# Preparation of a chunked RWKV-7 branch: wide matmuls between the chunk products, inverse and values on four array tiles, and a written order behind the inverse

## The chip, the cores and the metric

The kernel runs on one core of one Trainium2 chip. The metric is the device time of one execution in microseconds; a figure for a kernel is the median of its runs. Numbers of a trace are those of one profiled execution. The engines are named as in the profile: PE is TensorE's matmuls, PEld its weight loads, DVE VectorE, ACT ScalarE, POOL GpSimd, SP SyncE, which issues nearly all DMAs.

## The reference

One layer of a decoder on 1024 tokens of 1024 channels: three branches on one normalised input (causal pooling, RWKV-7, cross attention into 256 memory tokens), gates, an output projection, and a convolutional FFN. The change lies in the RWKV-7 branch, whose recurrence runs over tokens, with a 64x64 state in each of 16 heads:

```python
def step(state, inp):
    rt, wt, kt, vt, an, bn = inp
    sa = jnp.einsum('bhvk,bhk->bhv', state, an)
    state = state * wt[:, :, None, :] + sa[..., None] * bn[:, :, None, :] + vt[..., None] * kt[:, :, None, :]
    yt = jnp.einsum('bhvk,bhk->bhv', state, rt)
    return state, yt
...
kk = kk * lax.rsqrt(jnp.sum(kk * kk, axis=-1, keepdims=True) + L2_EPS)
w_log = -jax.nn.softplus(-(w0 + jnp.tanh(dw) @ w_up_decay).astype(f32)) - 0.5
a = jax.nn.sigmoid((a0 + da @ w_up_a).astype(f32))
```

## The kernel before, in words

Tokens are cut into 16 chunks of 64, so the recurrence becomes matrix products within a chunk, a triangular inverse per chunk and head, and a walk over the 16 chunks. Full precision comes from splitting each fp32 operand into a high and a low part: one product of a 128x128 weight tile with 512 tokens is a **wide triple**, three matmuls (`mm3`, lines 180 to 182). An fp32 operand that isn't split makes the chip run two matmuls for one in the code, so the trace counts twice what the code writes.

In time, the program is: the start; four **groups** of preparation (`rwkv_group`, two pairs of heads each, `i` = 0 and 1); the walk (`chain`); attention, pooling, gates and FFN. A group does, in the code's order:

- **lengths** (`square_sums`, 464 to 473): ACT squares the keys twice, once rounded into `sp[:, 0]` and once in full into a half of `tHV`; DVE subtracts the two into `sp[:, 1]`; PE sums over channels into `phd` (two matmuls a half, bank pool `pss`); ACT turns that into a reciprocal root, by Ln and Exp, back into `tHV` (`rstd`).
- **up-projections** (496 to 504): eight pairs of matmuls `psu`, each followed by a Sigmoid on ACT; then the table of activation functions goes back to Ln and Exp. The two banks of pool `g0` are shared with `in_block`.
- **r and scaling** (525 to 554): for each `i` a projection `in_block` of 48 wide matmuls, and some ten operations of DVE and ACT that make `AR`, `BK` and `kv`.
- **values** (`pv`, 570 to 581): 64x64 products with `cent` that centre the values into `HV`, then its store to HBM (`spill`).
- **chunk products** (`ps`, 588 to 610): for each `i` four bursts of four chunks. A burst writes two PSUM banks (`ps1`, `ps2`); ACT copies one half of each bank (605, 608) and DVE masks the rest out of them (606, 607, 609, 610). Four banks are rotated, so a third burst needs the banks of the first. Behind them stand a bonus (`pbo`), scaling and transposes (`pt`) and stores.
- **solve** (647 to 664): 31 steps on DVE invert the diagonal 32x32 blocks and end in eight copies into `NTu`, the last of which is `place`.
- **inverse** (`pz`, `pw`, 665 to 682): 32x32 products complete the 64x64 inverses, in two halves of 16 chunks: `pz`, a copy by ACT and one by DVE into `Z`, `pw`, copies by ACT into `NT`. `NT` is then stored (line 693, `d_nt`).

Two sources of wide triples that nothing near them needs fill PE under the solve: keys and values of the next group (`group_kv`, 64 triples a group), and the projections whose results are spilled for later (`fill_to`, 32 jobs of 16 triples, lines 861 to 888). `fill_to(48 * (g + 1))` asks for 48 more in each group. A scheduler then places all of this on the engines' queues by its own estimate of times; `later(a, b)` only says that `a` stands behind `b`.

SBUF buffers go by tags: two tiles with one tag share one slot, and a new tile's first write waits until all readers of the tile before it are done, its stores included. `tHV` and, after it, `HV` hold the slot "HV"; `NT` holds the slot "NT". In the walk, `pair` takes "HV" and `state` takes "NT".

Of the kernel before, what the change touches and what calls it, by code (L numbers as in the profile page):

```python
# [17 lines left out]
P = 128  # L18
# [3 lines left out]
C = 64  # L22
# [8 lines left out]
LAST = HK - 4  # L31

# [12 lines left out]
def trunk_kernel(ctx: ExitStack, tc: tile.TileContext, xT, memT, pvec, w_in, w_kv, w_upd, w_upg,  # L45
# [416 lines left out]
    def square_sums(src, scale, sq, sp):  # L462
# [6 lines left out]
        for n, (t0, _) in enumerate(HALVES):  # L469
            ps = pss.tile([P, 512], F32, name="phd", tag="s")  # L470
            PE.matmul(ps, bonesr, sp[:, 0, t0:t0 + 512], start=True, stop=False)
            PE.matmul(ps, bonesr, sp[:, 1, t0:t0 + 512], start=False, stop=True)
            yield slice(t0, t0 + 512), ps

    def rwkv_group(g, kv):
# [10 lines left out]

        def lengths():
            for i in range(2):
                for s, ps in square_sums(kv[i][:, 0], col("k_k", 2 * g + i), tHV[:, i, 1], sp[:, i]):
                    rstd(tHV[:, i, 1, s], ps, 1)  # L490

        if g:
            lengths()
            table(SIGMOID)
        for i in range(2):
            p = 2 * g + i
            uh, ul = load_up2(w_upd[p])
            for t0, _ in HALVES:
                s = slice(t0, t0 + 512)
                for e, l, dst, b in ((0, ld, tBN[i][:, 0, s], "w0"), (1, la, tHV[:, i, 0, s], "a0")):  # L500
                    ps = psg.tile([P, 512], F32, name="psu", tag="g0")
                    PE.matmul(ps, uh[:, e], l[:, s], start=True, stop=False)
                    PE.matmul(ps, ul[:, e], l[:, s], start=False, stop=True)
                    act(dst, ps, AF.Sigmoid, bias=col(b, p))
        table(LN_EXP)
        if g == 0:
            lengths()
        AR = rw.tile([P, 2, 3, T], F32, name="AR", tag="AR")
        vs = []
# [7 lines left out]

        for i in range(2):
            p = 2 * g + i
            t0_, t1_ = kv[i][:, 0], kv[i][:, 1]  # L520
# [13 lines left out]
            in_block(8 + p, shifted(p, r_))  # L534

# [18 lines left out]
            vs.append(t1_)  # L554

        def bonus(i):

            t0_ = kv[i][:, 0]
            for t0, _ in HALVES:
                s = slice(t0, t0 + 512)  # L560
                ps = pss.tile([P, 512], F32, name="pbo", tag="s")
                PE.matmul(ps, bones, t0_[:, s], start=True, stop=True)
# [7 lines left out]
        NT = rw.tile([P, 2, NCH, C], F32, name="NT", tag="NT")  # L570
        HV = rw.tile([P, 2, NCH, C], F32, name="HV", tag="HV")
        for i in range(2):
            for c0 in (0, 8):
                ps = pss.tile([P, 8, C], F32, name="pv", tag="s")
                for c in range(8):
                    tsl = slice((c0 + c) * C, (c0 + c + 1) * C)
                    PE.matmul(ps[64:128, c], vs[i][0:64, tsl], cent[0:64], start=True, stop=True)
                    PE.matmul(ps[0:64, c], vs[i][64:128, tsl], cent[64:128], start=True, stop=True)
                A.copy(HV[64:128, i, c0:c0 + 8], ps[64:128])
                A.copy(HV[0:64, i, c0:c0 + 8], ps[0:64])  # L580
            spill(d_hv, (g, i), HV[:, i])

# [6 lines left out]
        for i in range(2):  # L589
            us = slice(NCH * i, NCH * i + NCH)  # L590
            for c0 in range(0, NCH, 4):
# [5 lines left out]
                m = None  # L597
                for c in range(4):
                    t = slice((c0 + c) * C, (c0 + c + 1) * C)
                    for e, rows in ((1, up), (0, lo)):  # L600
                        m, was = PE.matmul(ps[e][:, c], BK[i][rows, c0 + c], AR[rows, i, e:e + 2, t],
                                           start=True, stop=True), m
                        if was is not None:
                            later(m, was.ins)
# [22 lines left out]
            for c0 in range(0, NCH, 4):  # L627
                ps = pss.tile([P, 4, P], F32, name="pt", tag="s")
                for c in range(4):
                    PE.transpose(ps[:, c], BK[i][:, c0 + c], ident)  # L630
# [27 lines left out]
        fill_to(48 * (g + 1))  # L658
        if g == 3:
            w_queue[0] = A  # L660
            fill_to(256, solve)
        for us in (slice(0, NCH), slice(NCH, 2 * NCH)):
            for q, (qs, bs) in enumerate(quads):
                place = V.tensor_copy(NTu[qs, us, bs], X[qs, us]).ins
        Z = tmp
        ends = [(slice(e, e + 32), slice(e + 32, e + 64)) for e in (0, 64)]
        for u0 in (0, 16):
            us = slice(u0, u0 + 16)
            ps = pss.tile([P, 16, 32], F32, name="pz", tag="s")
            for u in range(16):  # L670
                for q0, q1 in ends:
                    m = PE.matmul(ps[q1, u], NTu[q0, u0 + u, 32:64], S11[q0, u0 + u], start=True, stop=True)
                    if u0 == u == 0:
                        later(m, place)
            A.copy(Z[32:64, us], ps[32:64])
# [1190 lines left out]
```

## Time and profile before

| what | before |
|---|---|
| median of 3 runs | 1940.28 us (1934.13 to 1942.58) |
| profiled execution, its own time | 1933.07 us |
| its span | 1931.4 us |
| PE, DVE, ACT, POOL busy | 97%, 71%, 54%, 41% |
| the four groups, first to last | 94 us to 665 us of the span |
| the walk | 665 us to 858 us |

The profiled execution took 1.7 us more than its span, and lies 7.2 us under the median. In the trace "start us, us" are an instruction's start and duration; a bracket is the time that its engine sat idle before it and what ended that. A matmul's duration contains the array's latency, so the rate is read from the distance between starts.

### The profile page before, as it was taken

To read this page: it belongs to the slowest core of one execution; us is meant where nothing else is said; L and a number is where in the kernel's file an instruction comes from. 1 tells how busy PE (TensorE), PEld (TensorE's weight loads), DVE (VectorE), ACT (ScalarE), POOL (GpSimd) and SP (SyncE) were. 2 spreads that over 40 slices of the span, in tenths; PEclk is the share of its full clock that TensorE was granted. 3 is DMA by queue.
4 is the path that set the end of the run, shared out by engine and by line. 5 is a ranking of instruction groups with operands and counts; after the bars stand their busy time and mean duration, and the time that the engine had idled before them with its cause. 6 is when DMAs were issued, how large, how long until landed. Compare 5 with 4: busy or idle time off the path is not lost.

```text
span 1931.4 us, 33821 instructions
## 1 busy us (share of the span) xinstructions
PE 1869.7 (97%) x12204; PEld 1515.9 (78%) x12204; DVE 1366.2 (71%) x2054; ACT 1048.7 (54%) x2190; POOL 785.7 (41%) x867
## 2 busy tenths in 40 slices
PE   8999999998999999999999999999999999999997
PEld 6767877876777888788788888888788888888886
DVE  8677677677677446657964534679798888877798
ACT  6685385385484355555664345555454454544544
POOL 4422221222221211121323455566599888821441
PEclk9999999999999999999999999999999999999999
DMA  5326236326239669975246444653322222289775
GB/s 165 130 73 184 93 88 179 100 77 186 94 95 303 207 195 317 329 220 183 96 139 207 130 131 141 194 164 123 105 85 90 86 80 85 88 263 211 170 189 144
DMA packets 269641, 296.28 MB, mean 153 GB/s; under 512 B 18336, under 2 KB 219168, under 8 KB 266400
## 3 DMA queue, kind: packets, MB, share of 16 engines
q1 hardware_dynamic: 248480, 271.56, 44.5%
q0 software_dynamic: 11856, 14.16, 4.5%
q10 hardware_dynamic: 9136, 8.39, 1.5%
q8 instruction: 96, 1.57, 0.3%
q14 instruction: 73, 0.60, 0.1%
HBM read 207.00 MB, written 87.03 MB: 152 GB/s over the span
## 4 chain that ended last, share of the span: by engine, by line
PE 65%; DVE 5%; DMA 3%; ACT 1%; issue 1%; POOL 0%; SPq 0%; DVEq 0%; ACTq 0%; POOLq 0%
PE psg L180 11%; PE psg L182 11%; PE psg L181 11%; PE psf L182 6%; PE psf L180 6%; PE psf L181 6%; PE psd L181 3%; PE psd L182 3%; PE psd L180 3%; PE py L780 1%; DMA R<-d_f 1%; PE pr L780 1%; PE ph L780 1%; DMA hv<-d_hv 1%; DMA gt<-d_bv 1%
## 5 line engine op out<-in xcount | busy, mean ns | idle before, releaser
L139 POOL TENSOR_TENSOR wlo<-wraw,whi 128x256 fp32r<-128x256 f32 x464 | 403.9, 883 | 827.1 <-ACT whi L132 772.8
L180 PE MATMUL psg<-hh,whi 128*128 128x512 f32 x928 | 373.9, 403 | 12.7 <-ACT whi L132 8.5
L182 PE MATMUL psg<-hh,wlo 128*128 128x512 f32 x928 | 368.7, 398 | 1.6 <-POOL wlo L139 1.4
L181 PE MATMUL psg<-hl,whi 128*128 128x512 f32 x928 | 369.0, 398 | 0.3 <-DVE hl L266 0.2
L132 ACT CAST whi<-wraw 128x256 fp32r<-128x256 f32 x472 | 181.5, 403 | 246.1 <-PE psg L181 96.1
L180 PEld LDWEIGHTS psg<-hh,whi 128*128 128x128 f32 x928 | 175.7, 189 | 55.8 <-ACT whi L132 14.4
L182 PEld LDWEIGHTS psg<-hh,wlo 128*128 128x128 f32 x928 | 176.0, 190 | 42.6 <-POOL wlo L139 4.9
L181 PEld LDWEIGHTS psg<-hl,whi 128*128 128x128 f32 x928 | 176.0, 190 | 36.7 <-issue 1.4
L1192 POOL TENSOR_TENSOR wt<-a,wt 128x256 fp32r<-128x256 f32 x136 | 155.5, 1167 | 35.3 <-ACT wt L1191 35.3
L181 PE MATMUL psd<-f,u 128*128 128x512 f32 x292 | 114.0, 390 | 0.5 <-DVE f L1608 0.4
L180 PE MATMUL psd<-f,u 128*128 128x512 f32 x292 | 113.2, 391 | 1.2 <-ACT f L1604 1.2
L182 PE MATMUL psd<-f,u 128*128 128x512 f32 x292 | 113.7, 389 | 0.0
L182 PE MATMUL psf<-h2h,wt 128*128 128x512 f32 x272 | 105.9, 389 | 0.1
L180 PE MATMUL psf<-h2h,wt 128*128 128x512 f32 x272 | 105.9, 389 | 0.0
L181 PE MATMUL psf<-h2l,wt 128*128 128x512 f32 x272 | 105.8, 389 | 0.0
L1206 DVE SCALAR_TENSOR_TENSOR d<-z,pv,d 128x1023 f32<-128x1023 f32 x68 | 101.1, 1491 | 2.1
L1192 POOL TENSOR_TENSOR wt<-s,wt 128x256 fp32r<-128x256 f32 x68 | 81.2, 1213 | 2.8 <-ACT wt L1191 1.9
L181 PE MATMUL psf<-t,wt 128*128 128x512 f32 x204 | 79.4, 389 | 0.0
L180 PE MATMUL psf<-t,wt 128*128 128x512 f32 x204 | 79.4, 389 | 0.0
L182 PE MATMUL psf<-t,wt 128*128 128x512 f32 x204 | 79.4, 389 | 0.0
L1204 ACT ACTIVATE d<-z,pv 128x1024 f32<-128x1024 f32 x34 | 42.4, 1247 | 65.7 <-DVE z L1286 49.9
L1191 ACT CAST wt<-a 128x256 fp32r<-128x256 f32 x136 | 50.7, 404 | 40.8 <-POOL wt L1192 25.9
(436 smaller groups left out, 4499.2 us busy)
## 6 DMA issues: line engine op xcount, KB each, us to landing
wraw<-in_w_in SPq DMA_DIRECT2D x176, 128.0 KB, 2.4
a<-in_w_fup SPq DMA_DIRECT2D x128, 128.0 KB, 2.4
d_ar<-AR SPq DMA_DIRECT2D x24, 512.0 KB, 4.2
d_zg<-st SPq DMA_DIRECT2D x48, 256.0 KB, 3.5
ring<-d_ar SPq DMA_DIRECT2D x8, 1536.0 KB, 11.9
wraw<-in_w_fup SPq DMA_DIRECT2D x80, 128.0 KB, 2.5
fraw<-d_f SPq DMA_DIRECT2D x33, 256.0 KB, 4.1
d_rb<-RB SPq DMA_DIRECT2D x16, 512.0 KB, 5.7
```

The lines of the kernel that those rows point to most:

```text
L132: i = A.copy(hi, src)
L139: (V if lo_on_dve[0] else G).tensor_tensor(lo, src, hi.bitcast(F32), op=ALU.subtract)
L180: first = PE.matmul(ps, wh, xh, start=start, stop=False)
L181: PE.matmul(ps, wh, xl, start=False, stop=False)
L182: last_mm[0] = PE.matmul(ps, wl, xh, start=False, stop=stop).ins
L780: m = PE.matmul(out_, l, r, **kw)
L1191: A.copy(w[0][:, us], src[u])
L1192: low = eng.tensor_tensor(w[1][:, us], src[u], w[0][:, us].bitcast(F32), op=ALU.subtract)
L1204: A.activation(d, z, AF.Identity, scale=col("cw2", j), bias=col("cb", j))
L1206: V.scalar_tensor_tensor(d[:, n:], z[:, :T - n], col(cw, j), d[:, n:], op0=ALU.mult, op1=ALU.add)
```

## The change

1. **Values** move ahead: they are made after the `in_block` of `i` = 0 (new `values()`), all four quadrants of the array in turn, a half of the chunks in each of two banks, each product ordered behind the one before.
2. **Slots are swapped**: `HV` now takes the slot "NT", and `NT` takes the slot "HV", which it shares with `tHV`.
3. **Inverse**: the two halves of `pz`, and of `pw`, are interleaved, so that four 32x32 tiles take turns in one bank; the second stage is ordered behind the copies of the first.
4. **Chunk products**: a burst stands as one row, with one wide triple after the first and two after the second and third (`covered`); one triple stands ahead of each later bonus product and of four transposes in group 3.
5. **Behind the inverse**: four triples behind `place`, two within the lengths of `i` = 1, ten among the up-projections. For this 16 triples of groups 0 to 2 are left to the next group (`LEFT`); the sum stays 48 a group. In `square_sums` the order of the two products is turned.

The core of the diff:

```diff
+GROUP, LEFT = 48, 16
+TAKEN = 4 * GROUP + 64
...
         for n, (t0, _) in enumerate(HALVES):
             ps = pss.tile([P, 512], F32, name="phd", tag="s")
-            PE.matmul(ps, bonesr, sp[:, 0, t0:t0 + 512], start=True, stop=False)
-            PE.matmul(ps, bonesr, sp[:, 1, t0:t0 + 512], start=False, stop=True)
+            if n == 0 and ahead is not None:
+                wide = ahead()
+            m = PE.matmul(ps, bonesr, sp[:, 1, t0:t0 + 512], start=True, stop=False)
+            if n == 0 and ahead is not None:
+                later(m, wide)
+            last_sum_[0] = PE.matmul(ps, bonesr, sp[:, 0, t0:t0 + 512], start=False, stop=True).ins
...
+        cover, burst = [GROUP * g - LEFT if g else 0], [None]
+
+        def covered(n, behind=None):
+            cover[0] += n
+            fence[0] = behind
+            wide = fill_to(cover[0])
+            fence[0] = None
+            return wide
+
         if g:
+            covered(4, placed[0])
             lengths()
             table(SIGMOID)
+        raised = [0, last_sum_[0]]
...
-                    PE.matmul(ps, uh[:, e], l[:, s], start=True, stop=False)
-                    PE.matmul(ps, ul[:, e], l[:, s], start=False, stop=True)
+                    m = PE.matmul(ps, uh[:, e], l[:, s], start=True, stop=False)
+                    if g and 2 <= raised[0] < 7:
+                        later(m, covered(1 if raised[0] > 2 else 6, raised[1]))
+                    m = PE.matmul(ps, ul[:, e], l[:, s], start=False, stop=True)
+                    raised[:] = raised[0] + 1, m.ins if raised[0] > 1 else raised[1]
...
+        def values():
+
+            lo, up = slice(0, 64), slice(64, 128)
+            HV = rw.tile([P, 2, NCH, C], F32, name="HV", tag="NT")
+            after = last_mm[0]
+            for i in range(2):
+                ps = [pool.tile([P, 8, C], F32, name="pv", tag=tag)
+                      for pool, tag in (((psk, "k"), (psc, "c")) if i else ((pss, "s"), (pss, "s")))]
+                for c in range(8):
+                    for n in (1, 0):
+                        t = slice((8 * n + c) * C, (8 * n + c + 1) * C)
+                        for rows, at_ in ((lo, lo if n else up), (up, up if n else lo)):
+                            m = PE.matmul(ps[n][at_, c], vs[i][rows, t], cent[rows], start=True, stop=True)
+                            later(m, after)
+                            after = m.ins
+                for n in range(2):
+                    A.copy(HV[up, i, 8 * n:8 * n + 8], ps[n][lo if n else up])
+                    A.copy(HV[lo, i, 8 * n:8 * n + 8], ps[n][up if n else lo])
+                spill(d_hv, (g, i), HV[:, i])
+            return HV
...
             in_block(8 + p, shifted(p, r_))
+            if i == 0:
+                HV = values()
...
-        NT = rw.tile([P, 2, NCH, C], F32, name="NT", tag="NT")
-        HV = rw.tile([P, 2, NCH, C], F32, name="HV", tag="HV")
+        NT = rw.tile([P, 2, NCH, C], F32, name="NT", tag="HV")
...
-                m = None
+                after = covered(min(2, c0 // 4), burst[0]) if c0 else None
...
+                        if after is not None:
+                            later(m, after)
+                        after = m.ins
+                burst[0] = after
...
-        fill_to(48 * (g + 1))
+        fill_to(GROUP * (g + 1) - (LEFT if g < 3 else 0))
...
+        us = slice(0, 16), slice(16, 32)
+        ps = pss.tile([P, 16, 32], F32, name="pz", tag="s")
+        for u in range(16):
+            for h in range(2):
+                for ends_ in ends:
+                    m = PE.matmul(ps[ends_[1 - h], u], NTu[ends_[0], 16 * h + u, 32:64],
+                                  S11[ends_[0], 16 * h + u], start=True, stop=True)
...
+        for h in range(2):
+            moved = [A.copy(Z[32:64, us[h]], ps[ends[0][1 - h]]),
+                     V.tensor_copy(Z[96:128, us[h]], ps[ends[1][1 - h]])]
+        ps = pss.tile([P, 16, 32], F32, name="pw", tag="s")
+        for u in range(16):
+            for h in range(2):
+                for ends_ in ends:
+                    m = PE.matmul(ps[ends_[h], u], Z[ends_[1], 16 * h + u],
+                                  NTu[ends_[1], 16 * h + u, 32:64], start=True, stop=True)
+                    for i in moved:
+                        later(m, i.ins)
+        for h in range(2):
+            for ends_ in ends:
+                A.copy(NTu[ends_[0], us[h], 32:64], ps[ends_[h]])
...
-    chain(lambda v: 279 + 121 * (v - 1) // 46 if v else 262)
+    chain(lambda v: TAKEN + 23 + (377 - TAKEN) * (v - 1) // 46 if v else TAKEN + 6)
```

The last line yields the same numbers as before. Where the scheduler now puts the instructions is seen at three places. The rows are those of an engine's queue in the built program; numbers behind a name count buffers, and a name of a semaphore behind "waits" is an engine's or, with DMAHW, a DMA queue's.

First, PE at the first chunk products of group 1, before (a burst is eight rows of two banks' names; "..." leaves out its repeats):

```order
L181 MATMUL psg<-hl,whi 128x512
L601 MATMUL ps_2705<-AR,BK_2337 128x128
L601 MATMUL ps_2704<-AR,BK_2337 128x128
...
L601 MATMUL ps_2721<-AR,BK_2337 128x128
L601 MATMUL ps_2720<-AR,BK_2337 128x128
...
L182 MATMUL psg<-hh,wlo 128x512
L601 MATMUL ps_2737<-AR,BK_2337 128x128
```

And after the change, from the end of the first burst:

```order
L641 MATMUL ps_2702<-AR,BK_2255 128x128
L182 MATMUL psg<-hh,whi 128x512
L183 MATMUL psg<-hl,whi 128x512
L184 MATMUL psg<-hh,wlo 128x512
L641 MATMUL ps_2719<-AR,BK_2255 128x128
```

Before, two bursts stand together, then one wide matmul, then the next two; now 3, 8 and 6 wide matmuls stand between the bursts of `i` = 0, and 3, 6 and 6 for `i` = 1.

Second, ACT behind the inverse of group 0, before: the squares for group 1 stand far ahead, and the copies of the inverse are followed by Ln and Exp on `phd`.

```order
L467 ACTIVATE sp_2333<-kv1_1712,pv_88 128x512 [waits DVE_49,Activation_49]
L467 ACTIVATE tHV_2336<-kv1_1712,pv_88 128x512
...
L675 COPY tb1_1875<-pz_2261 32x512 [waits PE_49]
L682 COPY NT_1223<-pw_2296 32x16x32 [waits PE_49]
L682 COPY NT_1223<-pw_2296 32x16x32
L214 ACTIVATE tHV_2336<-phd_2345,eps_114 128x512 [waits PE_49]
```

After the change (the `sp` squares still stand ahead, the `tHV` ones don't):

```order
L723 COPY tb1_1937<-pz_2111 32x512 [waits DVE_49]
L735 COPY NT_1330<-pw_2180 32x16x32 [waits PE_49]
L735 COPY NT_1330<-pw_2180 32x16x32 x3
L471 ACTIVATE tHV_2254<-kv0_1611,pv_88 128x512 [waits DMAHW1_49,DMAHW0_49,Activation_49]
L471 ACTIVATE tHV_2254<-kv1_1774,pv_88 128x512 x2
L216 ACTIVATE tHV_2254<-phd_2300,eps_114 128x512 [waits DVE_49,PE_49]
```

The four squares into `tHV` have moved behind the copies into `NT`, and the first of them now waits for two DMA queues.

Third, PE at the same place, before:

```order
L680 MATMUL pw_2296<-NT_1223,tb1_1875 32x32 x30
L471 MATMUL phd_2345<-sp_2333,bonesr_95 128x512 [waits PE_49]
L472 MATMUL phd_2345<-sp_2333,bonesr_95 128x512
L182 MATMUL psg_3364<-hh_146,wlo_3348 128x512
L180 MATMUL psg_3364<-hh_146,whi_3353 128x512
```

After the change:

```order
L718 MATMUL pz_2111<-tb1_1937,NT_1330 32x32 x63
L182 MATMUL psg_2281<-hh_146,whi_2258 128x512 [waits Activation_49]
...
L729 MATMUL pw_2180<-NT_1330,tb1_1937 32x32 x60
L525 MATMUL psu_2340<-ld_219,uhi_2334 128x512
L528 MATMUL psu_2344<-la_220,ulo2_221 128x512
L477 MATMUL phd_2300<-sp_2251,bonesr_95 128x512 [waits DVE_49,PE_49]
L480 MATMUL phd_2300<-sp_2251,bonesr_95 128x512
```

The first sum of the lengths has stayed right behind the inverse, with two pairs of up-projections between; its wait now names DVE, whose subtraction needs the squares. Nine wide matmuls stand between `pz` and `pw`.

More of the change, by code (lines that the diff above doesn't have):

```diff
@@ L485, in rwkv_group, with between @@
         BKs = [rw.tile([P, NCH, P], F32, name=f"BK{i}", tag=tagB[i]) for i in range(2)]
+        def between():
+            return covered(2, last_sum_[0])
         def lengths():
             for i in range(2):
-                for s, ps in square_sums(kv[i][:, 0], col("k_k", 2 * g + i), tHV[:, i, 1], sp[:, i]):
+                for s, ps in square_sums(kv[i][:, 0], col("k_k", 2 * g + i), tHV[:, i, 1], sp[:, i],
+                                         between if g and i else None):
                     rstd(tHV[:, i, 1, s], ps, 1)
+        cover, burst = [GROUP * g - LEFT if g else 0], [None]
[5 more added lines that the diff above has]
+            return wide
         if g:
+            covered(4, placed[0])
             lengths()
             table(SIGMOID)
+        raised = [0, last_sum_[0]]
         for i in range(2):
@@ L507, in rwkv_group @@
             lengths()
+            covered(1)
         AR = rw.tile([P, 2, 3, T], F32, name="AR", tag="AR")
-        vs = []
+        vs = [kv[i][:, 1] for i in range(2)]
         turn = [0]
@@ L561, in bonus @@
                 ps = pss.tile([P, 512], F32, name="pbo", tag="s")
-                PE.matmul(ps, bones, t0_[:, s], start=True, stop=True)
+                m = PE.matmul(ps, bones, t0_[:, s], start=True, stop=True)
+                if g == 3 and (i or t0):
+                    later(m, covered(1, burst[0]))
+                burst[0] = m.ins
                 V.tensor_tensor(t0_[:, s], vs[i][:, s], ps, op=ALU.mult)
@@ L600, in rwkv_group @@
                     for e, rows in ((1, up), (0, lo)):
[L601 to L604, printed above, removed]
+                        m = PE.matmul(ps[e][:, c], BK[i][rows, c0 + c], AR[rows, i, e:e + 2, t],
+                                      start=True, stop=True)
+                        if after is not None:
+                            later(m, after)
+                        after = m.ins
+                burst[0] = after
                 A.copy(RB[i][:, 0, cs], ps[0][:, :, 1])
@@ L629, in rwkv_group @@
                 for c in range(4):
-                    PE.transpose(ps[:, c], BK[i][:, c0 + c], ident)
+                    m = PE.transpose(ps[:, c], BK[i][:, c0 + c], ident)
+                    if c == i == 0 and g == 3:
+                        later(m, covered(1, burst[0]))
+                burst[0] = m.ins
                 A.copy(BKN[i][:, c0:c0 + 4], ps)
@@ L875, in fill_steps @@
                     later(m, behind)
+                if fence[0] is not None:
+                    later(m, fence[0])
                 filled.append(last_mm[0])
```

38 lines of the change are left out of this document (8 added, 30 removed).

## The prediction

> **What bounds the kernel now.** I read the page's busy times first, then its chain of waits, then PE's busy time by stretches of group 1 and group 2, then the timeline of PE inside each stretch, with DVE's and ACT's beside it. The first two, from the page:
>
> ```profile
> span 1931.4 us, 33821 instructions
> PE 1869.7 (97%) x12204; PEld 1515.9 (78%) x12204; DVE 1366.2 (71%) x2054; ACT 1048.7 (54%) x2190; POOL 785.7 (41%) x867
> PE 65%; DVE 5%; DMA 3%; ACT 1%; issue 1%; POOL 0%; SPq 0%; DVEq 0%; ACTq 0%; POOLq 0%
> ```
>
> PE is the bound: 65% of the chain, and the next engine has 5%. But "busy" counts a matmul's latency, so I look at what a stretch achieves. The windows are: the inverse of group 1, from there to the first chunk product of group 2, its chunk products up to the solve, and the chunk products and solve of group 1 (PE busy and count, PEld, DVE, ACT, POOL, granted clock, DMA share, GB/s):
>
> ```profile
> 372.81:381.72 8.91, 8.91 (x273) 6.95 (x272) 1.39 (x2) 3.12 (x6) 0.72 (x1) 1.00 0.41 127
> 381.72:425.25 43.53, 42.64 (x293) 33.35 (x289) 30.69 (x32) 38.24 (x56) 11.74 (x11) 1.00 0.24 69
> 425.25:455.72 30.47, 24.95 (x195) 18.27 (x195) 17.38 (x36) 22.57 (x58) 2.92 (x4) 1.00 0.64 192
> 283.73:314.45 30.72, 25.74 (x196) 18.98 (x195) 18.20 (x38) 22.57 (x58) 2.93 (x4) 0.97 0.64 191
> 314.45:372.81 58.36, 57.53 (x257) 46.86 (x256) 51.22 (x101) 22.23 (x46) 19.61 (x26) 0.99 0.41 124
> ```
>
> Only the chunk products leave PE idle, about 5.5 us of 30.5. Under the solve PE is full, so every wide matmul moved out of there to a gap shortens the solve's stretch, until DVE's chain is late. The unit price of that is the pitch of wide matmuls; the prices of the small products stand in the same timeline:
>
> ```profile
> 420.65 0.39 PE L182 MATMUL psg<-hh,wlo 128*128 128x512 f32 x1
> ...
> 422.24 0.39 PE L180 MATMUL psg<-hh,whi 128*128 128x512 f32 x1
> 422.56 0.27 PE L577 MATMUL pv<-cent,kv 64*64 64x64 f32 x1
> ...
> 424.66 0.22 PE L577 MATMUL pv<-cent,kv 64*64 64x64 f32 x1
> 424.67 0.22 PE L578 MATMUL pv<-cent,kv 64*64 64x64 f32 x1
> 424.82 0.50 PE L181 MATMUL psg<-hl,whi 128*128 128x512 f32 x1
> 425.25 2.09 PE L601 MATMUL ps<-AR,BK 64*128 64x128 f32 x32
> ...
> 678.54 0.69 PE L780 MATMUL pu<-Rs,pair 64*64 64x64 f32 x32
> 679.16 0.50 PE L180 MATMUL psg<-hh,whi 128*128 128x512 f32 x1
> ```
>
> From 420.65 to 422.24 seven wide matmuls start, 0.227 us apart. Into a block of small ones and out of it the step is longer: 422.24 to 422.56 is 0.32, 424.82 to 425.25 is 0.43. I take 0.3 us for a block's two borders together.
>
> **Values: -9.7.** They are 128 matmuls in the trace, 64 pairs of two row tiles, a pair each 0.058 us (32 pairs and the way out fill the 2.26 us from 422.56 to 424.82; less 0.3 that is 1.9, or 0.06 a pair), so 3.8 us, in three blocks of about 0.3: 4.7 a group. After the change one block has quartets. The walk's `pu` works on four quadrants: 32 matmuls and the switch out in 0.62 us (678.54 to 679.16), which is 8 quartets of about 0.058. So 32 quartets are 1.9 us, with a border 2.2. The gain is 2.5 in groups 1 to 3. In group 0 the values lay in two blocks, and I take 2.2 there: 9.7.
>
> **Inverse: -10.4.** The 8.91 us of the window hold 273 matmuls: 4 `psu` (0.91), 11 wide ones (2.50), the rest (258, of which 256 are the inverse) takes 5.5. Its rate:
>
> ```profile
> 372.81 1.20 PE L672 MATMUL pz<-tb,NT 32*32 32x32 f32 x64
> 373.94 0.50 PE L502 MATMUL psu<-ld,uhi 128*128 128x512 f32 x1
> ```
>
> 64 matmuls in 1.13 us is 0.032 a pair, with about 0.1 of border: 128 pairs are 4.1, and five blocks about 1.4. As quartets, 64 of 0.032 are 2.05, with three blocks (the wide triples split `pw`) 0.85: 2.9. The gain is 2.6, four times: 10.4. The copies between `pz` and `pw` now all stand ahead of `pw`: two of DVE at half of the window's 1.39, two of ACT at half of the 1.17 quoted below, 2.6 if none overlap. Nine wide matmuls behind `pz` (2.0) and the three that follow `pw`'s first rows (0.7) cover them, so I cost them at nothing; bare they would cost 2.6 a group.
>
> **Chunk products: -14.4.** These rows are the bursts of group 2, first of `i` = 0, then of `i` = 1, and what DVE does at their start:
>
> ```profile
> 427.26 0.51 PE L182 MATMUL psg<-hh,wlo 128*128 128x512 f32 x1
> 429.17 1.16 PE L601 MATMUL ps<-AR,BK 64*128 64x128 f32 x16 [1.40 <-DVE AR L610]
> 430.92 1.16 PE L601 MATMUL ps<-AR,BK 64*128 64x128 f32 x16 [0.60 <-DVE AR L610]
> 432.85 1.10 PE L562 MATMUL pbo<-kv,bonesr 128*128 128x512 f32 x2 [0.33 <-DVE AR L610]
> 448.13 2.06 PE L601 MATMUL ps<-AR,BK 64*128 64x128 f32 x32
> 456.81 0.41 PE L630 MATMUL pt<-ident,BK 128*128 128x128 f32 x2 [0.59 <-DVE AR L610]
> ```
>
> ```profile
> 421.31 1.64 DVE L553 TENSOR_TENSOR AR<-AR,tBN 128x1024 f32<-128x1024 f32 x1
> 427.29 0.43 DVE L609 TENSOR_TENSOR NT<-ps,mstrict 64x256 f32<-64x256 f32 x1 [4.33 <-ACT RB L608]
> ```
>
> The four bursts of `i` = 0 take 7.60 us (425.25 to 432.85). Two wide matmuls lie in it, 0.45; 7.15 is bursts and waits. After the change 17 wide ones lie in it. Sixteen matmuls start over about 0.9 us, so with a border for each burst the four are 4.7; the third still waits some 1.2 for the masks of the first, since four masks of 0.43 are 1.74 and the fill before it is 11 x 0.227 = 2.5 and starts before the masks do. That makes 5.94 beside the 17: a gain of 1.2. For `i` = 1 it is 8.68 us (448.13 to 456.81) with 4 wide, 7.77 otherwise; after, 15 wide and 5.35 otherwise (the masks are clear of AR's work there): 2.4. Together 3.6 a group, 14.4. The wide matmuls themselves are not a gain: they are missing later.
>
> **The new wait: +20.1.** `tHV` now takes the slot in which `NT` was, so the first square into `tHV` waits until both stores of the previous group's `NT` have landed. Behind it on ACT stand all of Ln, Exp and the sigmoids; on PE the sum `phd` waits for it at the head of the queue. The rows, around the end of group 1's inverse (381.72):
>
> ```profile
> 381.72 0.50 PE L471 MATMUL phd<-sp,bonesr 128*128 128x512 f32 x1
> 394.95 0.40 PE L180 MATMUL psg<-hh,whi 128*128 128x512 f32 x1
> ```
>
> ```profile
> 381.82 1.17 ACT L682 COPY NT<-pw 32x512 f32<-32x512 f32 x2 [2.69 <-PE pw L680]
> 383.01 0.69 ACT L214 ACTIVATE tHV<-phd,eps 128x512 f32<-128x512 f32 x1
> ...
> 387.81 1.28 ACT L208 ACT_TABLE_LOAD   x1
> ```
>
> ```profile
> d_nt<-NT SPq DMA_DIRECT2D x8, 512.0 KB, 3.2
> L467 ACT ACTIVATE tHV<-kv,pv 128x512 f32<-128x512 f32 x16 | 11.4, 719 | 2.2 <-ACT whi L132 2.0
> L468 DVE TENSOR_TENSOR sp<-tHV,sp x16: 628/790/1223, 81.9 to 485.2; 128x512 fp32r<-128x512 f32 x16
> ```
>
> Before, `phd` starts as soon as the inverse ends, T; ACT's eight Ln and Exp fill T+1.3 to T+6.1, and the r products begin at T+13.2 (394.95). After: four copies by ACT, half of 1.17 each, end at T+2.4; the store lands 3.2 later, T+5.7; a square (0.72) makes it T+6.4, with issue up to T+6.9; DVE's subtraction (0.63 to 0.9) T+7.6; `phd` starts at T+7.7. Until then PE has the four matmuls of two `psu`, about 1.0, and idles some 6.6 us. On ACT, Ln and Exp then begin at T+8.2 and take 4.8, the table 1.28, the first sigmoid 0.69: T+15.0. The `psu` behind it rotate two banks, so the next six come in steps of a triple and a pair (5 x 0.227 = 1.14, I take 1.2): T+22.2, and only then does the first r product get its bank. From there PE has 96 wide matmuls of r (21.8), the values (2.2) and borders (0.6): the first chunk product starts at T+46.8. Before it starts at T+43.5, with 8 more wide matmuls ahead of it (1.8), the values' 2.5 (counted above) and without the four `psu` of 0.91 that lay in the inverse's window: like for like 40.1. The wait costs 6.7 at each of three boundaries (ahead of groups 1, 2 and 3): 20.1. Its ends: 4.5 a boundary, if two thirds of the idle remain, and 9.0, the whole shift of the r products.
>
> Beside that, the Trainium skill: "TensorE: Matmul & The Clock Gate", in its part on the clock gate, says that an idle window of about 3.4 us halves PE's clock until as long a busy one is through; by it each of the three idles would cost up to about 1.7 us more (an estimate from that page), and the sum would be -8, and the time 1932. No idle of before is that long in the groups; its chunk products, idle for 5 of 30 us in pieces up to 1.4, show 0.97 once and 1.00 once at 30.72 and 30.47 us, so at most 0.25 there.
>
> **Small costs: +1.3.** In group 0 the first bursts stand ahead of 36 wide matmuls of `i` = 1's projection, and BK's copies behind eight of the values': 0 to 3.3, I take 1.0. The walk's start: 0.3 (0 to 1).
>
> **The solve: 0.** DVE's last copies end before `pz` by:
>
> ```profile
> 217.53 4.78 DVE L664 COPY NT<-tb 32x512 f32<-32x512 f32 x8
> 364.88 3.48 DVE L664 COPY NT<-tb 32x512 f32<-32x512 f32 x8
> 231.30 1.20 PE L672 MATMUL pz<-tb,NT 32*32 32x32 f32 x64
> ```
>
> In group 0 that is 231.30 - 222.31 = 9.0 us, in group 1 372.81 - 368.36 = 4.45. After the change PE reaches `pz` 263 - 216 = 47 wide matmuls (10.7 us) sooner in group 0, and 239 - 221 = 18 (4.1) in group 1 (numbers of wide matmuls between the last burst and `pz`, counted in PE's order); but DVE no longer does the next group's four subtractions (4 x 0.8 = 3.2) in that stretch, and the bursts' masks end earlier. I leave it at nothing; the bound is 1.7 in group 0 and 1 in each of two groups, about 3.
>
> Sum: -9.7 - 10.4 - 14.4 + 20.1 + 1.3 = **-13.1 us**. The profiled execution took 1933.07, 1.7 more than its span, and lies 7.2 under the median of 1940.28; the change gives 1920 against the one, and **1927 against the median**, which I forecast.
>
> **Rivals.** A difference of 0.5%, 9.7 us, is about what a measurement of this kernel can tell from no change.
>
> *The tiles of the inverse don't overlap, since they write one bank.* `pz` and `pw` have all four tiles in one bank, and half the quartet shares the rows of the other half. Then only the borders are saved: 1.4 - 0.85 = 0.55 a group, 2.2 in place of 10.4, the sum -4.9, 1935: same. For it: nothing in this trace has four tiles in one bank at 32x32. Against it: two row tiles into one bank start 0.01 us apart at 424.66 and last 0.22 each. By the Trainium skill, "TensorEngine Tiling (Array Packing)", "Gotcha 1: PSUM Pressure", different row tiles cannot access one bank at the same time; that pair of rows speaks against the rule for two. Chance 0.13.
>
> *Evacuation bounds the chunk products.* If the bursts wait for masks and copies at their own pace, the wide matmuls between them only take the place of idle time that the next wait gives back: no 14.4, the sum +1.3, 1942: same. For it: each wait's releaser is DVE or ACT. Against: ACT is busy 22.57 of 30.47 us and DVE 17.38, so neither is full. Chance 0.13.
>
> *The wait is covered*, because the up-projections and the fill run on while ACT waits: without the 20.1, the sum is -33, 1907. Against it: PE's queue is in order, and `phd` stands at its head. Chance 0.07.
>
> *The store lands late, and the change is slower.* At T+2.4 the two stores meet the other traffic of that place, weights and up-projections. The same SP queue shows what landing can take:
>
> ```profile
> ring<-d_ar SPq DMA_DIRECT2D x8, 1536.0 KB, 11.9
> ```
>
> At 11.9 in place of 3.2 each of three boundaries is 8.7 longer: +26.1, the sum +13.0, 1953. It decides the sign from a landing of 3.2 + 13.1 / 3 = 7.6 us on, and is slower by over 0.5% from 10.8 on. For it: the wait is for the slower of two stores. Against: eight stores have a median of 3.2, and the DMA share in the window after the inverse is 0.24. Chance 0.09.
>
> **How the numbers follow.** The forecast has 0.58, the rivals 0.13, 0.13, 0.07 and 0.09. The forecast's own range comes from its bounds: the wait -6.6 to +6.9 (three times 4.5 and 9.0), the small costs -1.3 to +3, the solve 0 to +3, the bursts by half a term, 7: taken together, not all at one end, 1917 to 1936. Its faster part (below 1930.6) is about two thirds, 0.40; the rest is within 0.5%. With the covered wait 0.07, and a share of the first rival's spread 0.04, faster is 0.51; same is 0.39, of it 0.18 of the forecast; slower 0.10, the last rival and 0.01 of the second one's spread. The range leaves out the last rival and half of the covered wait: 1909 to 1944.
>
> **What would show it right or wrong.** In the profile after: `pv` as one block of about 2 us a group; `pz` and `pw` quartets 0.032 apart (0.064 is the first rival); 17 and 15 wide matmuls between bursts, with the idle ahead of the third below 1.5 us and little ahead of the fourth; an idle of about 6.6 us ahead of the first `phd` in groups 1 to 3, released by DVE's subtraction, with ACT's first square idle behind `d_nt`; a `d_nt` landing near 3.2; `pz` with no wait for `place`. The prediction fails if `phd`'s idle is below 4 or above 11, if the inverse's window doesn't shrink by 2 us, or if the masks take the bursts' gain.

## The result and the profile after

| kernel | median | ratio to the kernel before |
|---|---|---|
| before | 1938.09 us (1933.61 to 1942.58, 6 runs) | 1 |
| changed | 1959.36 us (1957.39 to 1966.55, 6 runs) | 1.0114 (1.0090 to 1.0139) |

The change makes the kernel 1.1% slower, some 21 us; the forecast was 1927, 13 us faster, with a range up to 1944. The profiled execution of the changed kernel is the slowest of its six, 1966.55 us; that of before, 1933.07, is shorter than any of the six runs in the table. So 12 of the 33 us between the two profiles are the spread of runs, and about 8 us lie behind the inverse of group 3, in code that the change doesn't touch. I therefore read the profiles stage by stage and take totals from the medians. Among the experiments below, one execution, the profiled one of `four` (2070.20 us), ran at a granted clock of 0.846; its times are not used.

The page of the changed kernel:

```profile
span 1964.8 us, 33837 instructions
PE 1865.4 (95%) x12204; PEld 1506.3 (77%) x12204; DVE 1363.7 (69%) x2054; ACT 1049.1 (53%) x2190; POOL 786.6 (40%) x867
PE 74%; DVE 12%; DMA 6%; ACT 6%; issue 2%; POOL 1%; SPq 0%; ACTq 0%; DVEq 0%; POOLq 0%
```

PE does the same work in 4 us less, over a span 33 us longer; DVE, DMA and ACT now have 24% of the chain, where they had 9%. The stretches of group 1 (columns as in the prediction): from the inverse of group 0 to the first chunk product of group 1, the chunk products of `i` = 0 with what follows, those of `i` = 1, the solve, the inverse.

```profile
227.30:276.04 48.74, 41.34 (x292) 32.55 (x284) 27.35 (x30) 40.37 (x60) 11.75 (x11) 0.89 0.30 87
276.04:307.23 31.19, 25.34 (x142) 17.92 (x141) 17.88 (x31) 16.63 (x39) 3.40 (x6) 0.89 0.48 143
307.23:320.10 12.87, 12.53 (x105) 9.64 (x105) 9.00 (x19) 11.02 (x29) 2.98 (x3) 1.00 0.46 150
320.10:371.85 51.75, 49.48 (x215) 39.33 (x214) 44.94 (x92) 16.45 (x35) 18.20 (x24) 1.00 0.39 115
371.85:377.58 5.73, 5.73 (x269) 4.54 (x269) 1.39 (x2) 1.97 (x4) 0.73 (x1) 1.00 0.31 101
```

The first two are the trouble: 7.4 and 5.9 us of idle PE, and a granted clock of 0.89. PE's timeline shows where. At the first sums of the lengths (the idle in the bracket, then the step from start to start):

```profile
228.10 0.40 PE L528 MATMUL psu<-la,ulo 128*128 128x512 f32 x1
235.33 0.76 PE L477 MATMUL phd<-sp,bonesr 128*128 128x512 f32 x1 [6.83 <-DVE sp L472]
235.89 0.63 PE L480 MATMUL phd<-sp,bonesr 128*128 128x512 f32 x1
236.32 0.63 PE L477 MATMUL phd<-sp,bonesr 128*128 128x512 f32 x1
...
```

```profile
235.33:240.59 5.26, 5.26 (x13) 4.08 (x14) 2.98 (x4) 3.49 (x6) 0.00 (x0) 0.50 0.00 0
```

PE waits 6.83 us, and then steps at 0.43 us instead of 0.23 for 5 us, in which the granted clock is 0.50. On ACT, what it waits for:

```profile
227.41 2.35 ACT L735 COPY NT<-pw 32x512 f32<-32x512 f32 x4 [2.60 <-PE pw L729]
233.74 2.56 ACT L471 ACTIVATE tHV<-kv,pv 128x512 f32<-128x512 f32 x4 [3.98 <-DMA d_nt<-NT]
```

The squares into `tHV` start 3.98 us behind the last copy into `NT`, when its stores have landed. And at the chunk products of `i` = 0:

```profile
275.73 0.39 PE L184 MATMUL psg<-hh,wlo 128*128 128x512 f32 x1
276.04 1.16 PE L641 MATMUL ps<-AR,BK 64*128 64x128 f32 x16
...
286.67 2.08 PE L641 MATMUL ps<-AR,BK 64*128 64x128 f32 x16 [5.44 <-DVE AR L652]
288.68 0.79 PE L182 MATMUL psg<-hh,whi 128*128 128x512 f32 x1
...
292.75 0.70 PE L610 MATMUL pbo<-kv,bonesr 128*128 128x512 f32 x1
```

The first row is the last r product. The third burst waits 5.44 us for a mask of the first, and is itself at half rate (2.01 us to the next start where the first takes 1.09). These two idles come in each of groups 1 to 3 (6.8 to 6.9, and 5.4, 5.4, 7.5).

### The profile page after: what moved, and what is told of

Its sections match the earlier page's. It is cut to its first block, busy times and chain, and to the rows that moved or that the text cites. A ratio compares the mean times of both kernels' runs of the same rounds, so it can differ in the third digit from the quotient of the medians.

```text
span 1964.8 us, 33837 instructions
## 1 busy us (share of the span) xinstructions
PE 1865.4 (95%) x12204; PEld 1506.3 (77%) x12204; DVE 1363.7 (69%) x2054; ACT 1049.1 (53%) x2190; POOL 786.6 (40%) x867
## 4 chain that ended last, share of the span: by engine, by line
PE 74%; DVE 12%; DMA 6%; ACT 6%; issue 2%; POOL 1%; SPq 0%; ACTq 0%; DVEq 0%; POOLq 0%
PE psg L182 14%; PE psg L184 13%; PE psg L183 13%; PE psf L184 5%; PE psf L182 5%; PE psf L183 5%; PE psd L183 3%; PE psd L182 3%; PE psd L184 3%; DVE tb L698 2%; DVE tb L700 1%; PE py L833 1%; DMA Q<-in_w_fdn 1%; DMA d_nt<-NT 1%; DMA d_bv<-kv 1%
## 5 line engine op out<-in xcount | busy, mean ns | idle before, releaser
L182 PE MATMUL psg<-hh,whi 128*128 128x512 f32 x928 | 380.0, 409 | 18.0 <-ACT whi L134 9.7
```

Source lines behind the costliest of these rows:

```text
L182: first = PE.matmul(ps, wh, xh, start=start, stop=False)
```

## The experiments

The kernel before was measured again beside each experiment, with a median between 1935.1 and 1935.8 us where the changed kernel had 1938.09 beside it. A ratio is to these runs, and compares experiments better than the medians do.

**1. The values' copies on ACT.** ACT and DVE ahead of that third burst, in the changed kernel:

```profile
271.79 0.58 ACT L562 COPY HV<-pv 64x512 f32<-64x512 f32 x1
...
273.47 1.25 ACT L596 ACTIVATE tHV<-tHV,oka,pv 128x1024 f32<-128x1024 f32 x1
...
277.68 1.05 ACT L599 COPY BK<-tBN 64x1024 f32<-64x1024 f32 x1 [1.95 <-DVE tBN L598]
...
279.82 1.02 ACT L134 CAST whi<-wraw 128x256 fp32r<-128x256 f32 x3
280.75 0.68 ACT L331 ACTIVATE AR<-psg,omu 128x512 f32<-128x512 f32 x1
```

```profile
274.75 1.23 DVE L597 TENSOR_TENSOR tHV<-tHV,kv 128x1024 f32<-128x1024 f32 x1 [4.36 <-ACT tHV L596]
...
281.46 0.28 DVE L335 SCALAR_TENSOR_TENSOR AR<-zc,pv,AR 128x1 f32<-128x1 f32 x1 [3.09 <-ACT AR L331]
...
284.90 0.41 DVE L648 TENSOR_TENSOR NT<-ps,mstrict 64x256 f32<-64x256 f32 x1
```

The last r product starts at 275.73; its blend (L331) runs at 280.75, DVE's scaling behind it, and the first mask at 284.90. Eight copies into `HV` are the first suspect. `hv_late`:

```diff
-                    A.copy(HV[up, i, 8 * n:8 * n + 8], ps[n][lo if n else up])
+                    held.append(A.copy(HV[up, i, 8 * n:8 * n + 8], ps[n][lo if n else up]))
...
-            A.activation(t4_, t4_, AF.Identity, scale=col("k_a", p), bias=oka[:, p:p + 1])
+            scaled = A.activation(t4_, t4_, AF.Identity, scale=col("k_a", p), bias=oka[:, p:p + 1])
+            for m in held if i else ():
+                later(m, scaled.ins)
```

> The changed kernel with one order added: the eight copies of the values into HV stand on ACT behind the Identity scaling for i = 1 (L596 of the changed kernel), ahead of which they stand in the changed kernel. Theory A: these copies (8 x 0.58 = 4.7 us) hold up the scaling for i = 1, so DVE makes AR late and the masks of the first burst, which stand behind that on DVE, are late too. Then the idle ahead of the third burst of i = 0 falls from 5.4 us to 1 to 2.5 in groups 1 to 3, the matmuls behind it run at full pitch again (about 2 us a group), and the time falls by 12 to 19 us, from 1959 to 1940 to 1947. Rival B: the bursts now stand right behind the last r product, and the scaling is late for them whatever ACT does: the idle stays above 4 us and the time falls by less than 5 us.

1960.02 us, ratio 1.0129 (1.0108 to 1.0149): nothing gained. The idle of groups 1 and 2 grew to 6.1 and 6.0 us. Theory A, as stated, falls. B's numbers came true, but not its reason, that the scaling is late whatever ACT does; ACT's timeline shows something else in the way:

```profile
276.01 1.01 ACT L134 CAST whi<-wraw 128x256 fp32r<-128x256 f32 x3
279.81 0.40 ACT L134 CAST whi<-wraw 128x256 fp32r<-128x256 f32 x1 [2.79 <-DMA wraw<-in_w_in]
280.12 0.68 ACT L331 ACTIVATE AR<-psg,omu 128x512 f32<-128x512 f32 x1
```

The copies are out of the way, and the blend is where it was: it now stands behind a cast that waits 2.79 us for weights of the next group's keys. In the kernel before (here group 2), ACT has the last blend as soon as its product is there, ahead of the cast that waits:

```profile
418.36 0.69 ACT L329 ACTIVATE AR<-psg,omu 128x512 f32<-128x512 f32 x1 [0.95 <-PE psg L182]
420.47 0.41 ACT L132 CAST whi<-wraw 128x256 fp32r<-128x256 f32 x1 [1.42 <-DMA wraw<-in_w_in]
```

**2. The blend ahead of the casts.** `blend` orders the casts of those weights, and one copy into BK, behind the last blend; `blend_hv` has `hv_late`'s order as well.

```diff
+            blend[0] = A.activation(d, ps, AF.Identity, scale=omu[:, m:m + 1]).ins
...
-            A.copy(BK[0:64, :, 64:128], c3(t2_)[0:64])
+            m = A.copy(BK[0:64, :, 64:128], c3(t2_)[0:64])
+            if i:
+                later(m, blend[0])
+                ahead_of[0] = blend[0]
...
         split_w(raw[:, :n], hi[:, :n], lo[:, :n])
+        if ps.c == 0 and ahead_of[0] is not None:
+            later(whis[-1], ahead_of[0], True)
```

> The changed kernel with two orders added on ACT: the casts of the weights that the next group's keys (in group 3: attention's keys and values) need, and one of the two copies into BK for i = 1, stand behind the last blend of r (L331 of the changed kernel), ahead of which they stand in the changed kernel. Theory C: this blend waits on ACT behind casts that wait for a DMA and a copy that waits for DVE, DVE's scaling waits for the blend, the masks of the first burst wait behind the scaling. One copy into BK stays ahead of the blend, so it moves from 280.75 to about 278.7, and the idle ahead of the third burst of i = 0 falls from 5.4 to about 3 us: 2 to 3 us in each of four groups, 1948 to 1952 in place of 1959. Rival: the scaling's own time on DVE holds the masks, the idle stays above 5 us and the time at 1957 or more.

1952.47 us, ratio 1.0089 (1.0074 to 1.0104), just above what C gives. In groups 1 and 2 the idle of 5.4 us became 1.90 ahead of a wide matmul, for a cast, and 1.10 ahead of the third burst: C's 3 us in two pieces. The third burst is still at half rate.

> Both orders on ACT together: the casts and the copy behind the last blend, and the eight copies of the values behind the scaling for i = 1 (as in hv_late). Theory C: hv_late alone gained nothing, since the blend then waited for the casts' DMA; with both, nothing that waits stands ahead of the blend. It starts right behind the last r product, DVE is through with AR some 4 us later, and the idle ahead of the third burst falls to between 0.5 and 1.5 us, with no half pitch behind it: (4.4 + 2.2) x 3 = 20 us off, 1936 to 1943. Rival: the two orders don't add, and the idle stays above 3 us, the time above 1948.

1941.30 us, ratio 1.0029 (1.0015 to 1.0043), inside the expectation. PE and ACT of `blend_hv` at that place:

```profile
280.61 1.16 PE L650 MATMUL ps<-AR,BK 64*128 64x128 f32 x16 [1.25 <-DVE AR L661]
281.70 0.50 PE L185 MATMUL psg<-hh,whi 128*128 128x512 f32 x1
```

```profile
272.95 1.04 ACT L609 COPY BK<-tBN 64x1024 f32<-64x1024 f32 x1
274.02 1.26 ACT L334 ACTIVATE AR<-psg,omu 128x512 f32<-128x512 f32 x2
```

Both blends now run at once, the idle is 1.25 us, and the burst has its full rate. So the delay in groups 1 and 2 was ACT's queue order, of two things in a row: the values' copies, and behind them the casts and one copy into BK. Moving the first gained nothing, moving the second 7 us by the medians (1959.36 to 1952.47) or 5 by the ratios, moving both 18 (1959.36 to 1941.30) or 16.

**3. The wait for the store.** `no_store_wait` keeps squares and root in `tBN`, whose slot is free once the inverse is through.

```diff
-                for s, ps in square_sums(kv[i][:, 0], col("k_k", 2 * g + i), tHV[:, i, 1], sp[:, i],
+                for s, ps in square_sums(kv[i][:, 0], col("k_k", 2 * g + i), tBN[i][:, 1], sp[:, i],
...
-                    rstd(tHV[:, i, 1, s], ps, 1)
+                    rstd(tBN[i][:, 1, s], ps, 1)
...
-            V.scalar_tensor_tensor(t5_, t0_, col("k_k", p), t5_, op0=ALU.mult, op1=ALU.mult)
+            V.scalar_tensor_tensor(t5_, t0_, col("k_k", p), t3_, op0=ALU.mult, op1=ALU.mult)
```

> The changed kernel with the squares and the reciprocal root kept in the second half of tBN, which is free there, and not in tHV: the first square no longer waits for the stores of NT, and tHV is first written by a sigmoid, some 8 us after the inverse. Theory: the idle ahead of the first sum of the lengths falls from 6.85 us to below 2.5 at each of the three boundaries, no matmuls at half pitch follow it (2.3 us each), and the time falls by 20 to 27 us, from 1959 to 1932 to 1939. Rival: the sigmoids and their two banks set the pace there, so that an idle of 4 us or more turns up ahead of the up-projections or the r products, and the time falls by less than 10 us.

1954.32 us, ratio 1.0100 (1.0085 to 1.0115): a gain as small as the rival's, but not where it put the loss. At the lengths the idle did go (two of 0.9 and 1.0 are left), but a new one stands before the inverse of groups 1 and 2. Its ACT, and its PE:

```profile
362.50 1.33 ACT L471 ACTIVATE tBN<-kv,pv 128x512 f32<-128x512 f32 x2 [7.99 <-DVE NT L709]
...
364.20 0.40 ACT L134 CAST whi<-wraw 128x256 fp32r<-128x256 f32 x1
```

```profile
364.66 0.79 PE L182 MATMUL psg<-hh,whi 128*128 128x512 f32 x1 [4.93 <-ACT whi L134]
```

My edit made this: the squares stood far ahead in ACT's queue, and now wait there 7.99 us for the solve to leave `tBN`'s slot, with a cast for PE behind them. `both` joins it with `hv_late`.

> Both edits of the two kernels before. If the two delays are apart in time and in cause, their gains add: 32 to 46 us below the changed kernel, 1913 to 1927, and so below the kernel before by 11 to 25 us. If they are one delay seen in two places (the late lengths make the scaling late), the gain is that of the larger alone, 20 to 27 us, 1932 to 1939.

1958.65 us, ratio 1.0121 (1.0105 to 1.0138). With the blend still behind the casts and the squares still ahead of a cast, the run tells neither theory from the other. `blend_hv_ns` has `blend_hv`'s orders, and the squares into `tBN` ordered behind one of ACT's copies of `pz`. By the code these are every second square, of both `i`:

```diff
+                m = A.activation(d, src[:, s], AF.Square, scale=scale)
+                later(m, late[0])
+                if n_sq[0] % 2 and zcopy[0] is not None:
+                    later(m, zcopy[0])
```

> The same with the wait for the store of NT taken away too: squares and root of the lengths in the second half of tBN, as in no_store_wait, and those for i = 0 now ordered behind ACT's copies of the inverse, so that they no longer hold up the casts on ACT (4.9 and 4.5 us of idle there). If the delays add, a further 6 to 7 us at each of three boundaries (6.85 less 1.9, and 2.3 of half pitch): 1915 to 1925, and so 0.5 to 1.2% below the kernel before. If DVE's solve becomes late when PE comes earlier, there is a wait for place ahead of pz of 2 us or more, and the time is 1930 or above.

**1923.06 us, ratio 0.9933 (0.9917 to 0.9949)**: faster than both kernels, 0.7% under the kernel before. The wait and what it brought, the half rate behind it included, cost 1941.30 - 1923.06 = 18.2 us, 6.1 at each of three boundaries. PE of `blend_hv_ns` behind the inverse of group 0:

```profile
226.07 0.50 PE L484 MATMUL phd<-sp,bonesr 128*128 128x512 f32 x1
...
228.59 0.50 PE L484 MATMUL phd<-sp,bonesr 128*128 128x512 f32 x1 [0.88 <-ACT NT L749]
228.93 0.40 PE L487 MATMUL phd<-sp,bonesr 128*128 128x512 f32 x1
```

**4. The half rate behind an idle.** `kept_busy` leaves the wait as it is, and gives PE something to do in it:

```diff
+            if n == 0 and ahead is None and placed[0] is not None:
+                for _ in range(26):
+                    later(PE.matmul(ps, bonesr, sp[:, 0, t0:t0 + 512], start=True, stop=True), inverse[0])
             m = PE.matmul(ps, bonesr, sp[:, 1, t0:t0 + 512], start=True, stop=False)
```

> The changed kernel with 26 extra matmuls of 512 columns behind the inverse of groups 0 to 2, into the bank that the first sum of the lengths then overwrites: they do nothing but keep PE busy through 5.9 us of the 6.85 us idle; the wait for the store stays. Clock theory: the 11 matmuls behind the wait that step at 0.43 us in the changed kernel step at 0.23 us, and the time falls by 2.3 us at each boundary, about 7 us, to 1952. Rival: the slow pitch comes from what these matmuls read or write: it stays at 0.43 us, and the time is the changed kernel's, 1959, or up to 3 us more.

1952.95 us, ratio 1.0087 (1.0065 to 1.0108), 6 us less than the changed kernel by the medians and 5 by the ratios. Its PE, and the stretch behind the wait:

```profile
228.01 6.32 PE L479 MATMUL phd<-sp,bonesr 128*128 128x512 f32 x26
...
235.98 0.50 PE L480 MATMUL phd<-sp,bonesr 128*128 128x512 f32 x1 [0.72 <-DVE sp L472]
...
```

```profile
235.98:241.24 5.26, 5.26 (x22) 4.09 (x23) 3.25 (x5) 5.24 (x10) 0.00 (x0) 1.00 0.01 3
```

The same matmuls with the same operands, which stepped at 0.43 us behind an idle PE, step at 0.23 to 0.36 behind a busy one, at a granted clock of 1.00. The idle itself is the cause of the slow rate there.

**5. The gains by themselves.** `inverse` is the kernel before with the inverse's new lines alone.

> The kernel before with the inverse alone changed: both halves interleaved, four 32x32 tiles taking turns in one bank, the second stage behind the copies of the first. The prediction's term: 5.5 us of PE become 2.9 in each of four groups, -10.4 us, 1925 by the 1935.6 of the kernel before. Rival (the tiles don't overlap in one bank): only two block borders a group are saved, -2.2 us, 1933. A second rival: the copies between the stages, now all ahead of the second one, are not covered by the few wide matmuls that the old order leaves there, and up to 2.6 us a group come back: no change.

1932.47 us, ratio 0.9987 (0.9973 to 1.0000). That is the time of the first rival, but by luck: the inverse takes what was forecast, and the gain is lost a stage later. A window of `inverse` over one inverse (4 `psu` and 8 wide matmuls in it, 0.9 and 1.8 us, so 3.0 for the rest, where 5.5 stood), and its PE and ACT ahead of the next chunk products:

```profile
373.61:379.34 5.73, 5.73 (x270) 4.55 (x269) 1.39 (x2) 1.97 (x4) 0.73 (x1) 1.00 0.32 104
```

```profile
423.46 0.27 PE L577 MATMUL pv<-cent,kv 64*64 64x64 f32 x1 [2.46 <-ACT HV L580]
```

```profile
422.24 0.58 ACT L579 COPY HV<-pv 64x512 f32<-64x512 f32 x1 [2.64 <-DVE kv L552]
```

The third block of values needs a bank whose copy into `HV` waits for DVE's last read of `tHV`. In the kernel before that block waited in group 3 alone, 1.9 us; now it waits 2.5, 2.5 and 2.1 us in groups 1 to 3. The inverse ended 2.4 us sooner (379.34 us for 381.72), but the copy is no sooner (422.24 for 421.31). Behind each of the three waits the granted clock is 0.50 for 3.4 us, which it isn't at that place in the kernel before. By the measure of the table further down, the stretches from the inverse to the chunk products are 8.7 us longer in these groups together, of 10 us that the four inverses gained. Neither rival of this run names it.

`four` adds the values on four quadrants in one block, at their old place.

> The kernel before with two parts of the change alone: the inverse with two halves interleaved, and the values on four quadrants in one block, at their old place (behind both r projections) and with the old slots; no wide triples are moved. The sum's terms: -9.7 for the values and -10.4 for the inverse, less up to 1 us a group where the first bursts wait for banks that the values held: 16 to 20 us below the kernel before, 1916 to 1920 by its 1936. Rival: both only move PE's waits, since DVE's solve ends when it did: less than 8 us.

1944.57 us, the middle one of its three other runs, ratio 1.0043 (1.0026 to 1.0059): slower than the kernel before, and the rival's side. Of its trace only the place of a wait is used: the first burst waits in each group for a copy into `HV`, as the one block now holds all four banks that the bursts need. Whether this is the whole loss was not tried.

`no_cover` is `blend_hv_ns` without triples between the bursts:

```diff
-                after = covered(min(2, c0 // 4), burst[0]) if c0 else None
+                after = burst[0] if c0 else None
```

> The kernel blend_hv_ns (both orders on ACT, no wait for the store) without the wide triples between the bursts: the four bursts of each i keep their one row, and the triples are asked for behind them, under the solve, as in the kernel before. The prediction's term for these triples is 3.6 us a group: 14.4 us more than blend_hv_ns, 1937. Rival: the bursts wait for masks whatever stands between them and the triples only shift PE's work, so that the time stays within 5 us of 1923.

1929.22 us, ratio 0.9971 (0.9958 to 0.9984): the triples between bursts are worth 6.2 us in this kernel (7.4 by the ratios), between the two expectations. Without them a cast is late for PE at the bursts of `i` = 0, and the third burst of `i` = 1 waits for masks (group 2):

```profile
414.71 0.49 PE L185 MATMUL psg<-hh,whi 128*128 128x512 f32 x1 [1.17 <-ACT whi L135]
...
437.46 1.16 PE L654 MATMUL ps<-AR,BK 64*128 64x128 f32 x16 [1.84 <-DVE AR L665]
```

## Why the prediction was wrong

**Values: the term was right in its stage.** In the changed kernel they are one block (this row, and the next start):

```profile
262.91 2.10 PE L557 MATMUL pv<-cent,kv 64*64 64x64 f32 x128
264.94 0.50 PE L182 MATMUL psg<-hh,whi 128*128 128x512 f32 x1
```

2.03 us where 2.2 was forecast. But the prediction costed the block's eight copies on ACT only for group 0, as "0 to 3.3, I take 1.0", and nowhere else. That was one part of the wrong step: they stand ahead of the scaling of `i` = 1 in every group.

**Inverse: right.** The rows of one stage:

```profile
371.85 1.29 PE L718 MATMUL pz<-tb,NT 32*32 32x32 f32 x128
373.07 0.50 PE L182 MATMUL psg<-hh,whi 128*128 128x512 f32 x1
```

128 matmuls in 1.22 us into one bank; the window of 5.73 less 12 wide ones (2.72) leaves 3.0, against 2.9 forecast. The rival "the tiles don't overlap" falls: four tiles, two of each row group, share a bank at the forecast rate. With it falls, for this case, the rule quoted there from the Trainium skill, "TensorEngine Tiling (Array Packing)", "Gotcha 1: PSUM Pressure". That 10.4 us of this would reach the end is not shown: alone it gave 2.7.

**Chunk products: the bursts right for `i` = 1, wrong for `i` = 0.** Of `i` = 1:

```profile
307.23 1.16 PE L641 MATMUL ps<-AR,BK 64*128 64x128 f32 x16
...
316.17 0.63 PE L672 MATMUL pt<-ident,BK 128*128 128x128 f32 x4 [0.26 <-DVE AR L652]
```

8.94 us less 15 wide matmuls (3.41) is 5.5, forecast 5.35. Of `i` = 0, 276.04 to 292.75 is 16.71, less 17 wide ones (3.86) 12.85, forecast 5.94. The failed step is "the third still waits some 1.2 for the masks of the first": it waited 5.44. The step needed the last blend to start right behind its product, as in the kernel before; but the last r product starts at 275.73 and the blend at 280.75, 5.0 us later. From there to the first mask it takes 4.2 us (284.90), where it took 4.6 before (from the blend at 418.36 to the end of its work on AR at 422.95). The order of ACT around the inverse was worked out; that around the r products was not. The 6.9 us above the forecast are 4.2 of waiting and most of the rest half rate, in each of groups 1 and 2, and more in group 3. Experiments 1 and 2 show the cause: undoing ACT's order took 16 to 18 us off.

**The wait: right as an idle; the clock beside it was left out.** `phd` starts at T+8.0 (235.33 - 227.3), forecast T+7.7, after an idle of 6.83, forecast 6.6. Taken away, it was worth 18.2, near the forecast of 20.1, but with the half rate in it, which the forecast didn't have: by `kept_busy` that is 5 to 6 of the 18. Eleven steps of 0.43 for 0.23 cost 2.2 us, and it happened at six idles, not at three: about 13 us in all, inside the amounts above. The sum left out the sentence that it gives beside it from the Trainium skill, "TensorE: Matmul & The Clock Gate". The prediction's own reading of idles "up to 1.4" was wrong, too; one of the windows that it shows holds these rows of the kernel before:

```profile
310.77 1.16 PE L601 MATMUL ps<-AR,BK 64*128 64x128 f32 x16 [1.79 <-ACT RB L605]
312.53 1.77 PE L601 MATMUL ps<-AR,BK 64*128 64x128 f32 x14 [0.60 <-ACT whi L132]
```

```profile
312.70:316.10 3.40, 3.40 (x22) 2.99 (x22) 3.23 (x6) 1.01 (x4) 0.63 (x1) 0.50 0.13 39
```

Behind them PE has half its clock for 3.4 us, and the window's end at 314.45 cut that in two.

**Group 0: too small.** PE waits 3.45 us there for a cast on ACT, and 1.04 for its low half, at the eight copies of the values; forecast 1.0. Behind them six wide matmuls step at 0.43, some 1.4 us more.

**The sum.** -13.1, and 6.9 x 3 for `i` = 0, 2 x 3 for the half rate at the lengths, 3.5 for group 0: +17 against a measured 21. With the waits that only group 3 has (7.5 in place of 5.4, and 1.99 at a transpose) that comes close to 21, but in part by luck, as the stages show. From each stretch of PE's time take 0.227 us for every matmul of 512 columns that starts in it, of which these three kernels have equally many; what is left is waits, borders, half rate and small products. Against the kernel before, in the profiled executions:

| stretches | forecast | changed | `blend_hv_ns` |
|---|---|---|---|
| group 0 up to its inverse | -4.8 | +1.2 | 0.0 |
| the four inverses | -10.4 | -10.0 | -10.0 |
| inverse to chunk products, groups 1 to 3 | +12.6 (-7.5 without the wait) | +17.0 | -4.7 |
| from the bursts of `i` = 0 to those of `i` = 1, groups 1 to 3 | -3.6 | +21.5 | +3.1 |
| from there to the inverse, groups 1 to 3 | -7.2 | -3.6 | -2.8 |
| behind the last inverse | +0.3 | +7.4 | +4.0 |

The bursts of `i` = 0 are the largest miss in the changed kernel, by 25 us. But the gains of group 0 did not come at all, and of that of `i` = 1, right in its bursts, half was gone before the inverse. Of the rivals, the one on the slower side had the sign, not the mechanism: the first square followed the copies after 3.98 us, so the store landed near its 3.2 (3.9 is the median of `d_nt` in the changed kernel) and far from 11.9.

What stays open: `blend_hv_ns` reaches the forecast's 13 us with the wait of 20 gone, so some 20 us of forecast gains did not come there either. By the last column they are missing in the bursts of `i` = 0 (6.7, of which 5.5 in group 3), in group 0 (4.8), between the bursts of `i` = 1 and the inverse (4.4), and ahead of the chunk products (2.8). Causes are shown for parts of it alone: the idles of 0.9 and 1.0 left at the lengths, and two later waits, 1.65 us for a cast and 2.2 for masks, in group 3. The 4.0 behind the last inverse are no more than the spread of these profiles there.

## What to carry to other kernels

An engine's in-order queue is a place of its own: when work moves, write down what it now stands ahead of on every engine that evacuates it, in each iteration and not only in the first, and what each of those instructions waits for. Two waits in a row on one queue hide each other, so an experiment that takes away one and finds no gain has not acquitted it; look at what ends the idle time then. A gain of PE's time ahead of a chain on other engines is worth only the slack of that chain.

## What was not expected of the hardware

PE steps at 0.43 us in place of 0.23 behind idles of 5.4 to 7.5 us, for 3.8 to 5.3 us, and does not when the idle is filled with matmuls whose result is thrown away (`kept_busy`). Behind a single idle of 1.25 us (`blend_hv`) it keeps its rate. In between no limit is shown: the granted clock is 0.50 for 3.4 us or more behind 2.46 us (`inverse`), behind 1.90 and 1.10 within four us (`blend`), and behind 1.79 and 0.60 in groups 0 and 1 of the kernel before, but not in its group 2. By the Trainium skill, "TensorE: Matmul & The Clock Gate", in its part on the clock gate, an idle window of some 3.4 us halves the clock until a busy one is through; the runs agree in kind, but here shorter idles did it too.
